# Making the MLP weight blocks elsewhere: none in the merge, two jobs fewer in the input stage, eight more in the first half of the MLP

## The chip, the cores and the metric

The kernel runs on one core of a Trainium2 chip. The metric is device time in microseconds (us). Before the change three runs took 2729.94, 2732.47 and 2736.2 us; the median is 2732.47.

The core has a matrix engine (PE, TensorE), and three engines for everything else: DVE (VectorE), ACT (ScalarE) and POOL (GpSimd). SP issues transfers; ACT and POOL can issue them as well. Matrix products land in PSUM banks and are taken out ("evicted") by DVE or ACT.

## What is computed

One layer of a transformer-like block on 2048 latent tokens of 1024 channels, with 256 context tokens. A token mixer (a Fourier part and a neighbourhood attention, gated and merged), then an MLP with a squared ReLU; both add to the residual stream. All is float32.

```python
hx = modulate(rms_norm(x, norm1_g), sh1, sc1)
fx, qx, kx, vx = split_projection(hx @ w_in)
...
y_four = fourier_mix(fx)
y_attn = neighbourhood_attention(qx, kx, vx, kc, vc, rpb)
mixed = gated_merge(hx, y_four, y_attn, w_branch_gate, w_fourier_out, w_attn_out, w_out)
x = x + g1 * mixed
hx2 = modulate(rms_norm(x, norm2_g), sh2, sc2)
a = relu(hx2 @ w_mlp1)          # 1024 -> 4096
x = x + g2 * ((a * a) @ w_mlp2) # 4096 -> 1024
```

## The kernel before

**Stages.** The program runs through the input projections (0 to about 850 us in the profiled execution), the Fourier transform along the tokens, attention (to about 1230), the merge (branch outputs, output projection, second norm; to 1530.8), and the MLP (to the end). Each float32 factor is split into a high and a low half of 16 bits, and a product is three matmuls (`mm3`, whose matmul stands on line 78).

**MLP.** Both matrix products are done by a Strassen-like scheme with 7 products in place of 8; a product is numbered c = 0 to 6. The tokens are cut in two halves. Each half goes through four groups of hidden channels (f = 0, 8, 16, 24). A group is a phase of the first product (mlp1: 4 units of 7 products, each of 12 matmuls, in PSUM tiles named pm) and then a phase of the second (mlp2: 7 products times 4 strips s of tokens, tiles named p): 336 matmuls of 128x512 each. In mlp1 every product is evicted by DVE or ACT into combinations u2, u3, u4, p1, which end as hidden tiles a (halves of 16 bits). In mlp2 it is added to accumulators X0 to X3 of its strip; the first one is written by ACT (line 1555), later ones are added by DVE (line 1551). mlp1 has four PSUM banks and mlp2 four others.

**Weight blocks.** The weights in this scheme are sums of quarters of the raw weight blocks. A *job* makes the 7 blocks of two neighbouring hidden tiles for w1 or w2: one load of raw weights (1 MB), 4 additions on DVE (`total`, line 414), and for each block a `put`: ACT makes the high half (line 375) and DVE the low half (line 376). Each block, 256 KB, is then stored to DRAM (w1d, w2d). There are 32 jobs. `prepare` is a generator that does one step at each `next`. Before the change 10 jobs are done in the input stage, at the end of the generator `side_work`, which `tick` advances between matmul groups there; 6 in the merge loop, whose steps stand between the parts of `out_proj` and `attn_out`; and 16 in the first half of the MLP, spread by the index of the product ("slot") up to a horizon. In the MLP there is one room for raw weights; the next 1 MB is fetched when a job is done. Its load is issued by ACT, the stores by POOL.

**Ring.** In both halves the MLP reads the blocks back through a ring of 15 tiles (wb), loaded by SP (line 1543) in the order of use. `issue_after` keeps the loads in this order. A load waits until PE is through with the tile that it overwrites.

**Normalised input.** The second norm writes its tiles (ho) to DRAM (hcd, line 1432), and the MLP reads the 7 combinations of them as tiles hc of 1 MB (line 1511): four (c = 0, 5, 6, 4) before the last token tiles are done, three (c = 1, 3, 2) after `norm_T` of the last tile has been issued in the program.

**Order.** Each engine runs its instructions in the program's order as a scheduler has placed them; transfers start in the order in which their issuing engine comes to them.

**The tail.** In the last group of a half the results are scaled (g2r), added to x (xr) and stored. The order of products in mlp2 is 0, 1, 4, 5, 2, 6, 3, so that c = 6 with six DVE instructions for each strip is next to last and c = 3 with two is last.

Of the kernel before, what the change touches and what calls it, by code (L numbers as in the profile page):

```python
# [8 lines left out]
F32 = mybir.dt.float32  # L9
# [10 lines left out]
D = 1024  # L20
# [16 lines left out]

PRODUCTS = (0, 5, 6, 4, 1, 3, 2)
PRODUCTS2 = (0, 1, 4, 5, 2, 6, 3)


# [18 lines left out]
def dit_block(ctx: ExitStack, tc: tile.TileContext, a, out, taps=None, upto=9):  # L60
# [223 lines left out]
    def side_work():  # L284
# [67 lines left out]
        for i, top in enumerate((BTOP, BTOP, BTOP, ATOP)):  # L352
# [8 lines left out]
        dve.tensor_scalar(out=g2r, in0=g2r, scalar1=msc[:, 4:5], scalar2=None, op0=ALU.mult)  # L361
        yield

        yield from prepare(jobs[:N_EARLY], lambda n_: pb.tile([128, KT, 256], F32, tag="awt", name=n_, bufs=2).rearrange("p k n -> p (k n)"),
                           lambda n_: pb.tile([128, 2, 256], F32, tag="aacc", name=n_, bufs=2).rearrange("p a n -> p (a n)"),
                           lambda n_: pb.tile([128, D], F32, tag="xh", name=n_, bufs=5)[:, :512].bitcast(F16).rearrange("p (o n) -> p o n", o=2),
                           sp.dma_start, sp.dma_start, True)
        del jobs[:N_EARLY]


    prepared, N_EARLY, N_MERGE = set(), 10, 6
    jobs = [(kind, f + o) for f in range(0, FF // 128, 8) for kind in (1, 2) for o in range(0, 8, 2)]
# [4 lines left out]

    def prepare(todo, raw_room, sum_room, out_room, load_, dma, ahead):

        todo, raws, out_ = list(todo), {}, []  # L380

# [14 lines left out]
        for n, (kind, f) in enumerate(todo):  # L396
# [8 lines left out]

            def put(c, src):
                flush()
                o = out_room(f"wo{nm}_{c}")
                d = o.rearrange("p o (k n) -> p o k n", k=4) if kind == 1 else o
                halve(d[:, 0], d[:, 1], src, msc[:, 0:1] if kind == 1 else msc[:, 2:3])  # L410
                out_.append(((w1d, w2d)[kind - 1][f // 2][c], o.rearrange("p o n -> p (o n)")))

# [4 lines left out]
            if kind == 1:  # L417
                order = ((0, b11, ()), (4, s3, (b21, b22, ALU.add)), (5, s3, (s3, b11)), (1, b12, ()), (6, b21, (b11, b21)),
                         (3, b22, ()), (2, s3, (b12, s3)))
            else:  # L420
                order = ((0, b11, ()), (4, s3, (b12, b11)), (5, s3, (b22, s3)), (2, b22, ()), (6, b12, (b22, b12)),
                         (1, b21, ()), (3, s3, (b21, s3)))
            for j, (c, o, ops) in enumerate(order):
                if ops:
                    total(o, *ops)
                put(c, o)
# [73 lines left out]
    def unit_T(wu, h, dst, m0, tk, func, name):  # L500
        w, u = wu
        for m in range(2):
            ps = mmp.tile([128, 512], F32, tag="mm", name=f"ps_{name}_{m}")
            ms = slice(m * 128, (m + 1) * 128)
            mm3(ps, [(w[:, 0, k, ms], w[:, 1, k, ms], h[:, 0, k], h[:, 1, k]) for k in range(KT)])
            put_T(ps, dst, m0 + m, tk, func, f"{name}_{m}", u[:, 1:2])
            tick()
            yield
# [31 lines left out]
    def unit_qk(wu, h, qk, p0, tk, t_rope, name):  # L540
# [66 lines left out]
        for i in range(nt):  # L607
            turned.append((back, i, front(i)))
            turn(3)
            tick()  # L610
            yield
# [6 lines left out]
    def unit_v(wu, h, u, tt, name):  # L618
        w, sc = wu
        und = sc[:, 1:2] if tt < 16 else sc[:, 2:3]  # L620
        for i in range(h.shape[3] // 128):
# [8 lines left out]
            sp.dma_start(vF[tt + i, :, u * 256:(u + 1) * 256], vo)  # L630
            tick()
            yield
# [228 lines left out]
    for n in range(len(seq)):  # L861
# [7 lines left out]
        if n == len(seq) - 1:  # L869
            for o in beside:  # L870
                for _ in o:
                    pass
# [596 lines left out]
    load_x1()  # L1469
    rooms = []  # L1470

    def block_room(i):

        if not rooms:
            rooms.append(pm.tile([128, 4, 512], F32, tag="mL", name="wrooms"))
        t = rooms[0][:, i]
        return t.bitcast(F16).rearrange("p (o n) -> p o n", o=2) if i else t

    turns = iter(range(1000))
    prep = prepare(jobs[:N_MERGE], lambda n_: pm.tile([128, 2048], F32, tag="mH", name=n_), lambda n_: block_room(0),  # L1480
                   lambda n_: block_room(1 + next(turns) % 3), sp.dma_start, pool.dma_start, False)
    for t in range(NT - 2):
        out_proj(t, 0)
        if t:
            next(prep, None)
        out_proj(t, 1)
        for _ in attn_out(t + 2, mmp, pg):
            if t:
                next(prep, None)
        if t:  # L1490
            next(prep, None)
        norm_T(t)
    for _ in prep:
        pass
    del jobs[:N_MERGE]
    pm.release()
# [20 lines left out]
    for half in range(2):  # L1517
        for f in range(0, NF, GF):
            pairs = tuple(range(f, f + GF, 2))
            slots += [(1, half, f1, c) for f1 in pairs for c in PRODUCTS]  # L1520
            slots += [(2, half, f, 0, s, pairs[:-1]) for s in range(4)] + [(2, half, f, 0, s, pairs[-1:]) for s in range(4)]
            slots += [(2, half, f, c, s, pairs) for c in PRODUCTS2[1:] for s in range(4)]

# [10 lines left out]
    def load_block():  # L1534
# [7 lines left out]
        with tc.issue_after(ring_load[0].ins) if ring_load[0] else nullcontext():  # L1542
            ring_load[0] = sp.dma_start(t.rearrange("p o n -> p (o n)"), (w1d, w2d)[kind - 1][f // 2][c])

# [100 lines left out]
    prep = prepare(jobs, lambda n_: pr.tile([128, 2048], F32, tag="raw", name=n_), lambda n_: pr.tile([128, 512], F32, tag="wt", name=n_),  # L1645
                   lambda n_: small(n_).bitcast(F16).rearrange("p (o n) -> p o n", o=2), act.dma_start, pool.dma_start, False)
    acc, banks = {}, {}

    def mlp2(half, f, c, s, pairs):
# [152 lines left out]
```

## Time and profile before

| | us |
|---|---|
| median of three runs | 2732.47 |
| the profiled execution | 2738.39 |
| its span | 2736.6 |
| PE busy | 2572.6 (94%) |
| DVE busy | 1813.5 (66%) |
| ACT busy | 1180.4 (43%) |
| POOL busy | 456.7 (17%) |
| mean granted clock of PE | 0.977 of full speed |

The profiled execution is one of its own; its span is the time between the first and last instruction on the core. A line of a wait says which engine stood idle before which instruction (output tile and line), and what ended the idle time. Releasers are inferred from semaphores: where an engine waits for several things, the last one is named. The times of all rows are those of this one execution.

### The profile page before, as it was taken

The page shows a single profiled execution, that of the slowest core. Times are in us where ns is not written, and L with a number is a line of the kernel's source. Part 1 is how long each engine was busy: PE and PEld are TensorE (multiplying, and loading weights), DVE is VectorE, ACT ScalarE, POOL GpSimd, SP SyncE. Part 2 cuts the span into 40 slices and gives each one's busy share as a digit, 9 for nine tenths or more (in the row PEclk, how much of TensorE's full clock was granted, in tenths as well). Part 3 has the DMA queues.
Part 4 walks back from the last instruction along what each step waited for, and adds up shares of the span by engine and source line. Part 5 has one row for each costly group of instructions (what it writes and reads, how often), then busy time and mean ns, then how long its engine had stood idle before and what let it go on. Part 6 is the DMA issues. An engine that isn't in the chain of part 4 may idle for free.

```text
span 2736.6 us, 42696 instructions
## 1 busy us (share of the span) xinstructions
PE 2572.6 (94%) x15825; PEld 1567.7 (57%) x15825; DVE 1813.5 (66%) x3628; ACT 1180.4 (43%) x2105; POOL 456.7 (17%) x688
## 2 busy tenths in 40 slices
PE   6899988898999799988999799999999999999998
PEld 5445756776746588877888444444444444444444
DVE  7746974667652678887896484877766743636367
ACT  5623326545331678873553372625342242414050
POOL 1201211012234454432120011111110100000000
PEclk9999999999999999999999999999999999999999
DMA  8577789777354655457987656655556533333334
GB/s 262 149 221 199 219 251 292 255 230 243 102 168 116 165 142 163 139 160 238 309 286 267 217 183 209 195 196 189 200 192 239 194 99 105 96 108 93 112 100 142
DMA packets 345514, 509.38 MB, mean 186 GB/s; under 512 B 48753, under 2 KB 210761, under 8 KB 340953
## 3 DMA queue, kind: packets, MB, share of 16 engines
q1 hardware_dynamic: 301897, 410.17, 48.2%
q0 software_dynamic: 27424, 69.72, 7.7%
q10 hardware_dynamic: 15984, 26.76, 3.0%
q8 instruction: 124, 2.03, 0.3%
q14 instruction: 85, 0.70, 0.1%
HBM read 361.72 MB, written 145.84 MB: 185 GB/s over the span
## 4 chain that ended last, share of the span: by engine, by line
PE 62%; DMA 14%; DVE 13%; issue 4%; ACT 4%; SPq 2%; POOL 1%; ACTq 0%; DVEq 0%; POOLq 0%
PE p L78 19%; PE pm L78 16%; PE ps_g L78 8%; PE po L78 4%; DMA w12m<-in_w_mlp 4%; DMA raw<-in_w_mlp 4%; PE tp L1259 2%; PE ps_k L78 2%; PE pmf L1197 2%; PE ps_f L78 2%; PE pv L1273 2%; SPq L178 1%; PE sc L1237 1%; PE pua L78 1%; DVE wo L376 1%
## 5 line engine op out<-in xcount | busy, mean ns | idle before, releaser
L78 PE MATMUL pm<-hc,wb 128*128 128x512 f16 x2688 | 585.5, 381 | 17.1 <-DMA hc<-hcd 12.5
L78 PE MATMUL p<-wb,a 128*128 128x512 f16 x2688 | 584.9, 380 | 10.4 <-DVE X L1551 5.5
L78 PEld LDWEIGHTS <-wb 128*128 128x128 f16 x2688 | 263.7, 98 | 337.3 <-issue 23.1
L78 PEld LDWEIGHTS <-a 128*128 128x128 f16 x2688 | 263.7, 98 | 330.3 <-issue 15.3
L78 PE MATMUL ps_g<-hx,w_g 128*128 128x512 f16 x1536 | 342.5, 380 | 0.7 <-ACT ot_f L497 0.7
L1551 DVE TENSOR_TENSOR X<-X,p 128x512 f32<-128x512 f32 x280 | 184.2, 685 | 219.7 <-PE p L78 194.1
L78 PEld LDWEIGHTS <-hx 128*128 128x128 f16 x2304 | 230.0, 100 | 45.3 <-issue 9.4
L78 PEld LDWEIGHTS <-w_g 128*128 128x128 f16 x1536 | 150.9, 99 | 170.9 <-issue 2.7
L1551 DVE TENSOR_TENSOR u<-pm,u 128x512 f32<-128x512 f32 x128 | 87.9, 690 | 94.0 <-PE pm L78 91.6
L1025 POOL DMA_DIRECT2D bt<-tT x264 | 132.4, 508 | 79.0 <-DVE ri L1266 58.7
L1246 DVE CUSTOM_DVE_ANT_0 s<-sc,bt,qsc 128x736 f32<-128x736 f32 (+5 forms) x128 | 111.2, 869 | 38.6 <-PE sc L1240 35.1
L1555 ACT ACTIVATE p<-pm 128x512 f32<-128x512 f32 x32 | 19.0, 593 | 253.5 <-PE pm L78 253.5
L375 ACT ACTIVATE wo<-raw,msc 128x512 f16<-128x512 f32 x104 | 71.6, 712 | 114.1 <-DMA raw<-in_w_mlp 67.8
L78 PE MATMUL po<-wouH,mH 128*128 128x512 f32 x256 | 103.0, 405 | 15.2 <-DVE ga L1316 15.2
L375 ACT ACTIVATE wo<-ws,msc 128x512 f16<-128x512 f32 x78 | 56.2, 720 | 140.6 <-DVE ws L414 91.3
L1267 DVE SCALAR_TENSOR_TENSOR pL<-tp,pH 128x640 f16<-128x640 f32 (+1 forms) x128 | 112.3, 877 | 6.7 <-ACT pH L1262 6.5
L497 ACT ACTIVATE ot_g<-ps_g,usc_g 128x512 f32<-128x512 f32 x64 | 43.6, 683 | 169.3 <-PE ps_g L78 155.4
L1682 POOL DMA_DIRECT2D xr<-x1d x32 | 17.3, 539 | 569.3 <-DVE X L1551 562.6
L1250 ACT ACTIVATE s<-s,m 128x736 f32<-128x736 f32 (+5 forms) x128 | 104.4, 816 | 15.9 <-DVE m L1246 15.5
L1259 PE MATMUL tp<-ident,s 128*128 128x128 f32 x704 | 104.3, 282 | 2.2 <-ACT s L1250 2.0
L78 PE MATMUL po<-wouH,mL 128*128 128x512 f32 x256 | 102.2, 401 | 0.0
L78 PE MATMUL po<-wouL,mH 128*128 128x512 f32 x256 | 102.2, 400 | 0.0
(511 smaller groups left out, 4778.5 us busy)
## 6 DMA issues: line engine op xcount, KB each, us to landing
wb<-w1d SPq DMA_DIRECT2D x224, 256.0 KB
wb<-w2d SPq DMA_DIRECT2D x224, 256.0 KB
w12m<-in_w_mlp SPq DMA_DIRECT2D x32, 1024.0 KB
gT<-ot_g SPq DMA_DIRECT2D x64, 256.0 KB
raw<-in_w_mlp SPq DMA_DIRECT2D x16, 1024.0 KB
raw<-in_w_mlp ACTq DMA_DIRECT2D x16, 1024.0 KB
hc<-hcd SPq DMA_DIRECT2D x14, 1024.0 KB
w1d<-wo POOLq DMA_DIRECT2D x56, 256.0 KB, 2.7
```

Of the source, the lines that this page charges most:

```text
L78: last_mm[0] = pe.matmul(ps, l, r, start=(start and i == 0), stop=(stop and i == n - 1))
L178: last_load[0] = sp.dma_start(dst, src)
L375: act.activation(hi, src, AF.Copy, scale=scale)
L497: act.activation(o, ps, func, scale=scale)
L1025: load_(t[i * 16:(i + 1) * 16, :, off + j0 * w:off + (j0 + 8) * w], raw(tT[ct], (2 * hp * 15 + dr) * w, [[120 * w, 16], [15 * w, 2], [1, 8 ...
L1197: pe.matmul(ps, l, r, start=(i == 0), stop=(i == len(prods) - 1))
L1246: tail["dve"] = dve.tensor_tensor_reduce(out=s[:, :n], in0=sc, in1=bias, op0=ALU.add, op1=ALU.min, scale=qsc[:, 4:5], scalar=3.0e38, accum ...
L1250: tail["act"] = act.activation(s[:, :n], s[:, :n], AF.Exp, bias=m1[:, 0:1], scale=-1.0, accum_out=m1[:, 1:2])
L1259: tail["pe"] = pe.transpose(tp[:, i * 128:(i + 1) * 128], s[:, o:o + 128], ident)
L1267: tail["dve"] = dve.scalar_tensor_tensor(out=pL[:, :c], in0=tp[:, :c], scalar=PTOP, in1=pH[:, :c], op0=ALU.mult, op1=ALU.subtract)
L1273: tail["pe"] = pe.matmul(pv, p_[:nk, i * 128:(i + 1) * 128], vv[:nk, h2 * 128 + o:h2 * 128 + o + 64], start=(j == 0 and i == 0), stop=(j = ...
L1551: last["dve"] = dve.tensor_tensor(out=o, in0=x, in1=y, op=op)
```

## The change

No job is made in the merge any more. 8 jobs are made in the input stage by a generator of its own (`early_blocks`), which starts when the side work is through and is paced by shares given to `tick`; two blocks share a room and a store there, so a job takes 4 stores. 24 jobs are made in the first half of the MLP, spread by the matmuls of a slot (`cost`) in place of its index, with two raw rooms; the next raw weights are fetched at the second put of a job. Blocks lie in DRAM in the order in which they are made (`MADE`). The ring has 13 tiles. The three late hc loads come ahead of the ring loads that follow (`ring_load` is set to the last of them). The first X3 of a strip is written by DVE. In the last group the order of mlp2's products is 0, 4, 5, 2, 6, 1, 3.

```diff
+MADE = {1: (0, 4, 5, 1, 6, 3, 2), 2: (0, 4, 5, 2, 6, 1, 3)}
 PRODUCTS2 = (0, 1, 4, 5, 2, 6, 3)
+PRODUCTS2F = (0, 4, 5, 2, 6, 1, 3)
...
-        yield
+    def early_blocks():
         yield from prepare(jobs[:N_EARLY], ...
-                           sp.dma_start, sp.dma_start, True)
+                           2, sp.dma_start, sp.dma_start)
-    prepared, N_EARLY, N_MERGE = set(), 10, 6
+    prepared, N_EARLY = set(), 8
...
-            def put(c, src):
-                flush()
-                o = out_room(f"wo{nm}_{c}")
+            def put(j, src):
+                if j % n_out == 0:
+                    flush()
+                    room[:] = [out_room(f"wo{nm}_{j}")]
+                    end = min(j + n_out, 7)
+                    out_.append(((w1d, w2d)[kind - 1][f // 2][j:end].rearrange("c p n -> p c n"), room[0][:, :end - j]))
+                o = room[0][:, j % n_out].rearrange("p (o n) -> p o n", o=2)
...
-                if j == 1 and ahead:
+                if j == 1:
                     fetch(n + 1)
                 yield
-            if n + 1 == len(todo):
-                flush()
-            elif not ahead:
-                fetch(n + 1)
-                yield
+        flush()
...
+    blocks = [early_blocks(), 0.0, False]
-    def tick():
+    def tick(share):
...
                 for o in beside:
-                    next(o, None)
+                    if next(o, o) is o and o is side:
+                        blocks[2] = True
+            if blocks[2]:
+                blocks[1] += share
+                while blocks[1] >= 1.0:
+                    blocks[1] -= 1.0
+                    next(blocks[0], None)
...
-    prep = prepare(jobs[:N_MERGE], ..., sp.dma_start, pool.dma_start, False)
     for t in range(NT - 2):
         out_proj(t, 0)
-        if t:
-            next(prep, None)
         out_proj(t, 1)
         for _ in attn_out(t + 2, mmp, pg):
-            if t:
-                next(prep, None)
-        if t:
-            next(prep, None)
+            pass
         norm_T(t)
-    for _ in prep:
-        pass
-    del jobs[:N_MERGE]
...
-    RING, GF = 15, 8
-    def load_hc(half, part):
+    RING, GF = 13, 8
+    def load_hc(half, part, then=None):
...
-            sp.dma_start(r[c].rearrange("p s o k t -> p s (o k t)"), hcd[half][c])
+            i = sp.dma_start(r[c].rearrange("p s o k t -> p s (o k t)"), hcd[half][c])
+        if then:
+            then[0] = i
...
-    hcs[0].update(load_hc(0, 1))
+    hcs[0].update(load_hc(0, 1, ring_load))
...
-    prep = prepare(jobs, lambda n_: pr.tile([128, 2048], F32, tag="raw", name=n_), ...
+    prep = prepare(jobs, lambda n_: pr.tile([128, 2048], F32, tag="raw", name=n_, bufs=2), ...
...
-                acts(X[x], ps, scale=-1.0 if op == ALU.subtract else 1.0)
+                if (c, x) == (0, 3):
+                    last["dve"] = dve.tensor_copy(X[x], ps)
+                else:
+                    acts(X[x], ps, scale=-1.0 if op == ALU.subtract else 1.0)
...
-    todo, steps = 8 * len(jobs), 0
-    horizon = next(i for i, s in enumerate(slots) if s[:4] == (2, 0, NF - GF, 0)) - RING
+    todo, steps, done = 7 * len(jobs), 0, 0
+    cost = [4 if s[0] == 1 else len(s[5]) for s in slots]
+    horizon = sum(cost[:next(i for i, s in enumerate(slots) if s[:4] == (2, 0, NF - GF, 0)) - RING])
...
-            while steps * horizon < i * todo and next(prep, "end") is None:
+            done += cost[i]
+            while steps * horizon < done * todo and next(prep, "end") is None:
                 steps += 1
```

On SP, at the passage from the merge to the MLP, these instructions stand in a row before the change: the last stores of x (x1d), four ring loads (wb) of the unit f = 4, and the first two of the late hc loads (hc0_1 is c = 1 of the first half).

```order
L1400 DMA x1d_76<-x1_1792_18434 128x1024
L1400 DMA x1d_76<-x1_1920_18497 128x1024
L1543 DMA wb1_0_4_5_18883<-w1d2_81 128x1024
L1543 DMA wb1_0_4_6_18885<-w1d2_81 128x1024
L1543 DMA wb1_0_4_4_18893<-w1d2_81 128x1024
L1543 DMA wb1_0_4_1_18900<-w1d2_81 128x1024
L1511 DMA hc0_1_18877<-hcd0_77 128x4096
L1511 DMA hc0_3_18879<-hcd0_77 128x4096
```

In the changed kernel the same place on SP reads so (line numbers are those of the changed kernel):

```order
L1412 DMA x1d_76<-x1_1792_18149 128x1024
L1412 DMA x1d_76<-x1_1920_18212 128x1024
L1503 DMA hc0_1_18592<-hcd0_77 128x4096
L1503 DMA hc0_3_18594<-hcd0_77 128x4096
L1503 DMA hc0_2_18596<-hcd0_77 128x4096
L1538 DMA wb1_0_2_2_18598<-w1d1_80 128x1024
L1538 DMA wb1_0_4_0_18606<-w1d2_81 128x1024
L1538 DMA wb1_0_4_5_18615<-w1d2_81 128x1024
```

The hc loads have moved ahead of the ring loads, and the ring loads behind them are four blocks earlier in the stream.

On DVE, at the start of the MLP, the last tile of the norm (ho7) is followed before the change by these (raw1_16 are the first raw weights of the MLP, ws their sum, wo a block, pm0_0_1 the product c = 1 of the first unit, p1 where it is added):

```order
L1431 TENSOR_TENSOR ho7_1_18865<-tm7_18805,ho7_1_18865 128x512
L1551 TENSOR_TENSOR a0_0_3_18926<-a22_0_0_18804,a0_0_3_18926 128x512
L414 TENSOR_TENSOR ws1_16_18889<-raw1_16_18887 128x512
L376 SCALAR_TENSOR_TENSOR wo1_16_0_18890<-raw1_16_18887,msc_139,wo1_16_0_18890 128x512
L376 SCALAR_TENSOR_TENSOR wo1_16_4_18897<-ws1_16_18889,msc_139,wo1_16_4_18897 128x512
L1551 TENSOR_TENSOR p1_0_0_18746<-pm0_0_1_18907,p1_0_0_18746 128x512
```

And in the changed kernel:

```order
L1443 TENSOR_TENSOR ho7_1_18580<-tm7_18520,ho7_1_18580 128x512
L1546 TENSOR_TENSOR a0_0_3_18652<-a22_0_0_18519,a0_0_3_18652 128x512
L423 TENSOR_TENSOR ws1_8_18602<-raw1_8_18600 128x512
L423 TENSOR_TENSOR raw1_8_18600<-raw1_8_18600 128x4x128
L381 SCALAR_TENSOR_TENSOR wo1_8_0_18603<-raw1_8_18600,msc_139,wo1_8_0_18603 128x512
L381 SCALAR_TENSOR_TENSOR wo1_8_1_18610<-ws1_8_18602,msc_139,wo1_8_1_18610 128x512
L1546 TENSOR_TENSOR p1_0_0_18461<-pm0_0_1_18633,p1_0_0_18461 128x512
```

Four instructions in place of three that need the first raw weights stand ahead of the eviction of the product; the raw weights are now those of an earlier group, f = 8.

## Rows read from the trace of the kernel before

**Rows 1.** Windows of four stretches: busy us and instructions by engine, clock, DMA, GB/s.

```profile
490.00:720.00 230.00, 211.70 (x1580) 158.32 (x1578) 167.60 (x417) 109.43 (x195) 29.92 (x31) 0.96 0.70 227
...
1252.50:1530.80 278.30, 265.76 (x1457) 230.41 (x1458) 210.25 (x404) 130.35 (x223) 40.41 (x59) 0.97 0.80 273
...
1573.10:2003.90 430.80, 419.85 (x1921) 188.99 (x1921) 306.35 (x476) 193.50 (x307) 55.97 (x104) 0.99 0.60 195
2003.90:2729.00 725.10, 725.10 (x3360) 328.55 (x3358) 413.54 (x639) 216.49 (x343) 29.70 (x55) 1.00 0.42 133
```

**Rows 2.** Waits of PE, 490 to 720: us in total, times, longest.

```profile
PE pu_g L475 <- DVE usc_k L476: 7.6, 2, 4.3
PE ps_k0c L78 <- DVE qn_k L558: 5.3, 1, 5.3
PE ps_v L78 <- ACT vo_v L627: 3.1, 2, 1.8
```

**Rows 3.** Waits of PE, 1252 to 1530 us.

```profile
PE po L78 <- DVE ga L1316: 15.2, 5, 7.0
PE tpb L1418 <- DVE tm L1423: 3.6, 1, 3.6
```

**Rows 4.** Waits of PE, 1525 to 1945 us.

```profile
PE pm L78 <- DMA hc<-hcd: 12.5, 3, 9.9
PE p L78 <- DVE X L1551: 5.5, 2, 4.1
PE p L78 <- ACT X L1555: 4.9, 1, 4.9
PE pm L78 <- DVE p L1551: 4.0, 1, 4.0
```

**Rows 5.** Waits of DVE, 1252.5 to 1530 us.

```profile
DVE wrooms L414 <- DMA raw<-in_w_mlp: 11.6, 5, 3.7
...
DVE wrooms L376 <- ACT wrooms L375: 3.5, 6, 1.1
```

**Rows 6.** Chain that ended last: start us, us, what.

```profile
1276.92 7.87 DMA raw<-in_w_mlp
```

**Rows 7.** Timelines of the MLP's start: start, us, engine, line, instruction, idle before.

```profile
1533.45 8.09 SPq L1543 DMA_DIRECT2D wb<-w1d  x4
1547.53 8.12 SPq L1511 DMA_DIRECT2D hc<-hcd  x3
...
1554.06 4.29 PE L78 MATMUL pm<-hc,wb 128*128 128x512 f16 x12 [9.92 <-DMA hc<-hcd]
...
1557.09 0.52 ACTq L387 DMA_DIRECT2D raw<-in_w_mlp  x1
...
1570.17 0.69 DVE L414 TENSOR_TENSOR ws<-raw 128x512 f32<-128x512 f32 x1 [11.16 <-DMA raw<-in_w_mlp]
...
1572.33 0.68 DVE L1551 TENSOR_TENSOR p<-pm,p 128x512 f32<-128x512 f32 x1
1572.92 0.68 DVE L414 TENSOR_TENSOR ws<-ws,raw 128x512 f32<-128x512 f32 x1
```

**Rows 8.** Timeline of DVE: two puts in a row, in the merge.

```profile
1292.22 0.75 DVE L376 SCALAR_TENSOR_TENSOR wrooms<-wrooms,msc 128x512 f16<-128x512 f32 x1
1292.88 0.75 DVE L376 SCALAR_TENSOR_TENSOR wrooms<-raw,msc,wrooms 128x512 f16<-128x512 f32 x1
```

**Rows 9.** Timeline of PE: the longest stall of the merge.

```profile
1252.52 0.77 PE L78 MATMUL po<-wouH,mH 128*128 128x512 f32 x1 [6.98 <-DVE ga L1316]
```

**Rows 10.** Waits of DVE, 1573 to 2003.9 us.

```profile
DVE wo L376 <- ACT wo L375: 32.5, 28, 3.3
```

**Rows 11.** Waits of ACT, 1690 to 2003 us.

```profile
ACT wo L375 <- DMA raw<-in_w_mlp: 32.8, 7, 5.8
```

**Rows 12.** Timelines of PE and DVE at the end.

```profile
2719.82 9.23 PE L78 MATMUL p<-wb,a 128*128 128x512 f16 x42
...
2732.39 0.69 DVE L1551 TENSOR_TENSOR X<-X,t 128x512 f32<-128x512 f32 x1
```

More of the change, by code (lines that the diff above doesn't have):

```diff
@@ L361, in side_work @@
         dve.tensor_scalar(out=g2r, in0=g2r, scalar1=msc[:, 4:5], scalar2=None, op0=ALU.mult)
[L362 removed]
+    def early_blocks():
         yield from prepare(jobs[:N_EARLY], lambda n_: pb.tile([128, KT, 256], F32, tag="awt", name=n_, bufs=2).rearrange("p k n -> p (k n)"),
                            lambda n_: pb.tile([128, 2, 256], F32, tag="aacc", name=n_, bufs=2).rearrange("p a n -> p (a n)"),
[L366 to L367 removed]
+                           lambda n_: pb.tile([128, D], F32, tag="xh", name=n_, bufs=5).bitcast(F16).rearrange("p (c n) -> p c n", c=2),
+                           2, sp.dma_start, sp.dma_start)
         del jobs[:N_EARLY]
[L371 removed]
+    prepared, N_EARLY = set(), 8
     jobs = [(kind, f + o) for f in range(0, FF // 128, 8) for kind in (1, 2) for o in range(0, 8, 2)]
@@ L376, in halve, with prepare @@
         dve.scalar_tensor_tensor(out=lo, in0=src, scalar=scale, in1=hi, op0=ALU.mult, op1=ALU.subtract)
-    def prepare(todo, raw_room, sum_room, out_room, load_, dma, ahead):
-        todo, raws, out_ = list(todo), {}, []
+    def prepare(todo, raw_room, sum_room, out_room, n_out, load_, dma):
+        todo, raws, out_, room = list(todo), {}, [], []
         def fetch(n):
@@ L417, in prepare @@
             if kind == 1:
-                order = ((0, b11, ()), (4, s3, (b21, b22, ALU.add)), (5, s3, (s3, b11)), (1, b12, ()), (6, b21, (b11, b21)),
-                         (3, b22, ()), (2, s3, (b12, s3)))
-            else:
-                order = ((0, b11, ()), (4, s3, (b12, b11)), (5, s3, (b22, s3)), (2, b22, ()), (6, b12, (b22, b12)),
-                         (1, b21, ()), (3, s3, (b21, s3)))
-            for j, (c, o, ops) in enumerate(order):
+                order = ((b11, ()), (s3, (b21, b22, ALU.add)), (s3, (s3, b11)), (b12, ()), (b21, (b11, b21)), (b22, ()), (s3, (b12, s3)))
+            else:
+                order = ((b11, ()), (s3, (b12, b11)), (s3, (b22, s3)), (b22, ()), (b12, (b22, b12)), (b21, ()), (s3, (b21, s3)))
+            for j, (o, ops) in enumerate(order):
                 if ops:
                     total(o, *ops)
-                put(c, o)
+                put(j, o)
                 if j == 0 and n:
                     prepared.add(todo[n - 1])
-                if j == 1 and ahead:
+                if j == 1:
                     fetch(n + 1)
                 yield
-            if n + 1 == len(todo):
-                flush()
-            elif not ahead:
-                fetch(n + 1)
-                yield
+        flush()
         prepared.add(todo[-1])
@@ L506, in unit_T @@
             put_T(ps, dst, m0 + m, tk, func, f"{name}_{m}", u[:, 1:2])
-            tick()
+            tick(1.5)
             yield
@@ L609, in unit_qk @@
             turn(3)
-            tick()
+            tick(0.6)
             yield
@@ L630, in unit_v @@
             sp.dma_start(vF[tt + i, :, u * 256:(u + 1) * 256], vo)
-            tick()
+            tick(0.8)
             yield
@@ L869, in dit_block @@
         if n == len(seq) - 1:
-            for o in beside:
+            for o in beside + blocks[:1]:
                 for _ in o:
@@ L1469, in dit_block @@
     load_x1()
[L1470 to L1481, printed above, removed]
     for t in range(NT - 2):
         out_proj(t, 0)
-        if t:
-            next(prep, None)
         out_proj(t, 1)
         for _ in attn_out(t + 2, mmp, pg):
-            if t:
-                next(prep, None)
-        if t:
-            next(prep, None)
+            pass
         norm_T(t)
-    for _ in prep:
-        pass
-    del jobs[:N_MERGE]
     pm.release()
@@ L1521, in dit_block @@
             slots += [(2, half, f, 0, s, pairs[:-1]) for s in range(4)] + [(2, half, f, 0, s, pairs[-1:]) for s in range(4)]
-            slots += [(2, half, f, c, s, pairs) for c in PRODUCTS2[1:] for s in range(4)]
+            slots += [(2, half, f, c, s, pairs) for c in (PRODUCTS2 if f + GF < NF else PRODUCTS2F)[1:] for s in range(4)]
     def blocks_of(s):
@@ L1639, in dit_block @@
     p2p = psum("mlp2", 4)
-    hcs[0].update(load_hc(0, 1))
+    hcs[0].update(load_hc(0, 1, ring_load))
     def small(name):
         return pr.tile([128, 512], F32, tag="wo", name=name, bufs=5)
-    prep = prepare(jobs, lambda n_: pr.tile([128, 2048], F32, tag="raw", name=n_), lambda n_: pr.tile([128, 512], F32, tag="wt", name=n_),
-                   lambda n_: small(n_).bitcast(F16).rearrange("p (o n) -> p o n", o=2), act.dma_start, pool.dma_start, False)
+    prep = prepare(jobs, lambda n_: pr.tile([128, 2048], F32, tag="raw", name=n_, bufs=2), lambda n_: pr.tile([128, 512], F32, tag="wt", name=n_),
+                   lambda n_: small(n_).bitcast(F16).rearrange("p (c n) -> p c n", c=1), 1, act.dma_start, pool.dma_start)
     acc, banks = {}, {}
```

3 lines of the change are left out of this document (1 added, 2 removed).

## Prediction, made before the changed kernel was run

> **What bounds the kernel now.** I read the windows first [rows 1]. From 2003.9 us to its end TensorE (PE) never waits: 3360 matmuls in 725.1 us, 0.2158 us each, so a phase of 336 lasts 72.5 us. Nothing done before 2003.9 can shorten that, except the few us behind PE's last matmul. What can go is PE's idle time before it. The waits of PE show where it lies near this change: 16 us in the input stage between 490 and 720 us [rows 2], 18.8 us in the merge [rows 3], and 27 us from the start of the MLP to 1945 us [rows 4]. In each the last releaser is an instruction of VectorE (DVE) or ScalarE (ACT), or one transfer. The chain and the waits of DVE then say what these engines were late with: raw weights and the blocks made of them [rows 5, 6].
>
> A stall costs more than its length. The twelve matmuls behind the 9.92 us stall took 4.29 us [rows 7]; at 0.2158 us they take 2.59. [...]
>
> **Input stage (two jobs fewer, evenly, fewer stores).** One block job is 7 puts (one ACT, one DVE instruction each), 4 DVE totals, a load of 1 MB and 1.75 MB of stores. Two puts on DVE start 0.66 us apart [rows 8], two plain operations 0.6 (1572.33 and 1572.92 in [rows 7]), so a job is 7 x 0.66 + 4 x 0.6 = 7.0 us of DVE. Two jobs less are 14 us of DVE, 14 puts of ACT and 5.5 MB, in a stretch where DVE is busy 168 of 230 us and DMA 70% [rows 1]; stores fall from 70 to 32. The waits on usc_k, qn_k and vo_v (16 us, and up to three clock losses, 5 us) are for short DVE and ACT instructions queued behind the block work. All of that but two clock losses is the one end, -18. The other is +4: the last jobs now stand nearer to the end of the stage, and one more stall like those of vo_v, with its clock loss, may come. I take -7, nearer the middle, since the side work that fills DMA there stays.
>
> **Merge (no jobs).** 6 jobs go: 42 us of DVE, and the 15.1 us that DVE stood waiting for raw weights and for ACT's half of a put [rows 5]. Of the 18.8 us, the longest stall, 7.0, ended at 1252.5 [rows 3, 9], and the first raw load that the chain runs through began at 1276.9 [rows 6]; that stall stays. Left are 15.2 - 7.0 + 3.6 = 11.8 us, and three clock losses, 5.1 us: at most -17. DVE is busy 210 of 278 us there and loses a fifth of it, and PE, which waits for its ga and tm, is busy 266 of the 278. The other end is -5, one stall with its clock loss: DMA is busy for 80% of the stretch, and what carries the tiles of this loop stays. I take -13, since the raw waits stood in front of PE's own evictions.
>
> **Start of the MLP.** PE waited 12.5 us for three tiles of normalised input (hc), 3 MB, and 4.0 us for p [rows 4]. The hc loads were issued from 1547.53 on, behind four block loads issued from 1533.45 on, each of which waits until PE is through with an older block [rows 7]. In the new order they stand ahead of those, right behind the last store of x, so they can start where the block loads did, 14 us sooner: the 12.5 us and one clock loss go. But what is late next is close. DVE's eviction of p (1572.33) stands behind three instructions that need the first raw weights, which landed at 1570.17, 13 us after their issue at 1557.09 [rows 7]. The new order has four there. PE has four banks and stops after as many products. The raw load's issue still stands behind the stores of the last norm tile. With hc out of the way those stores finish some 4 us sooner and the load needs about the 7.87 us of the chain [rows 6]: landing near 1561, 10 us earlier. From the landing to where the first mlp2 product needs its accumulator DVE has 104 instructions now, some 9 more, which is 5.4 us later. Net -5. The ends: -14, if the load's issue comes sooner with the shorter merge tail too; and +3, if the landing hardly moves.
>
> [...]
>
> **First half of the MLP (24 jobs where 16 were, two raw rooms).** 8 jobs more are 56 us of DVE, of which the order puts most where DVE has room: in the mlp2 phases, 48, 67, 68, 84 DVE instructions become 72, 85, 85, 84; in the mlp1 phases, 119, 100, 99, 82 become 128, 107, 109, 89. The first need at most 53 us of 72.5. The second bind: by 0.6 and 0.66 us they were 73, 62, 61 and 50 us and become 79, 66, 68 and 55, in a stretch of some 78 us (72.5 and what the banks let PE run ahead), and their ends were late by 4.9, 1.4 and 4.1 us already [rows 4]. The second and third group get 4.6 and 6.6 us more work. Against that stand DVE's waits for ACT's half of a put, 32.5 us, behind ACT's waits for raw weights, 32.8 us [rows 10, 11]: with a second room the next 1 MB is fetched two puts into a job instead of after it, 8 us or more ahead. I take 0 for the two groups; the ends are -5.5 (both late ends gone) and +11 (all waits stay, 4.6 + 6.6). DMA gets 8 x 2.75 MB more over 430 us, 195 to some 246 GB/s, in a stretch where it was busy 60%; at the merge's 273 GB/s it was 80%. The ring shrinks from 15 to 13 blocks; in mlp1 that is 13 x 2.59 = 34 us of lead, and in mlp2, with four in use, 9 x 2.59 = 23 us, against some 8 us for a load four times a block's size. I give it nothing.
>
> On what one DVE instruction costs, starts are 0.59 us apart (1572.33, 1572.92) while one lasts 0.68 [rows 7]. [...] The rows say that the next starts inside that time.
>
> **Tail.** PE ends at 2729.05 and DVE's last instruction at 2733.08 [rows 12]; it works off a queue, as the second to last product (c = 6) gives it 6 instructions in each strip, 4 x 6 x 0.6 = 14.5 us for 10.4 us of PE. Now a product with 3 (7.3 us) stands between that and the last one, and the queue is empty when the last begins: -2.5 (ends -0.5 and -2.7). The first X3 of each strip moves from ACT to DVE: some 20 instructions after 2003.9, where DVE is busy 414 of 725 us [rows 1]: nothing.
>
> **The sum** against the profiled execution's own 2738.4 us (span 2736.6 and 1.8 around it): -7 - 13 - 5 + 0 - 2.5 = -27.5, so 2710.9. That execution is 5.9 us above the median of the runs, 2732.5; on that basis 2705.
>
> **Rivals.** (a) *More than that.* Nothing is late next: merge -17, input -12, start -14, tail -2.5: -45.5, 2687. For it: every wait named has block work ahead of it in its engine's queue. Against: the norm tile's stores still stand before the raw load.
> (b) *The merge and the input stage were held by their own transfers.* DMA at 80% and 70% for it; DVE's waits for raw weights against it. Then 0 - 5 - 5 - 2.5: -12.5, 2720. If the early jobs are not done by the ticks and are drained in one go ahead of attention, it comes to the same number.
> (c) *Slower: block work on DVE and ACT sets the pace of the first three mlp1 phases.* 24 jobs where 16 were, and if each put waits for ACT as long as now, 32.5 us become 49, +16; all waits stay, +11; the start's gain is used up, +5; three stalls more than 3 us long lose the clock, +5. Together +37 on the forecast, 2742. For it: DVE has 66 to 79 us of work in 78. Against: two raw rooms. It decides from some 27 us of new waits on DVE or ACT between 1560 and 1950 us. [...] I count it here, with a chance of 0.03, since the starts speak against it.
>
> **How the numbers follow.** Forecast 0.50 (own range 2695 to 2716), (a) 0.15, (b) 0.18, (c) 0.17. A difference of 0.2%, 5.5 us, is about what a measurement can tell. Faster: the first three less a few hundredths, 0.80; within: those and a part of (c), 0.07; slower 0.13. The range, 2686 to 2738, reaches to (a) and up to (b) with the unknown ends of the MLP's terms (+3, +11).
>
> **What would show it.** In the merge no waits of DVE on raw, and PE's waits on ga and tm after 1277 mostly gone. No wait of PE on hc; the three loads issued right behind the last store of x; the first raw weights landing some 10 us closer behind PE's first mlp1 product. At the first mlp2 product of the first three groups PE waits of 5 us or less. No PE wait on wb, and none in the second half. DVE's last instruction 1 to 2 us behind PE's. It is wrong if the merge keeps over 8 us of such waits, or if PE's waits on X, u and p between 1560 and 2000 us exceed 20 us.

## The result

The changed kernel takes 2700.35 us (median of 4 runs, 2696.91 to 2706.24) against 2733.02 before (median of 4, 2729.94 to 2736.2): ratio 0.9883, 95% interval 0.9862 to 0.9904. It is 32.7 us faster; the forecast was 2705, and the range held it. The profiled execution took 2706.24 us, with a span of 2704.4.

The two profiled executions, cut at the same places of the program (us):

| stretch | forecast | before | after | difference |
|---|---|---|---|---|
| start to PE's first output projection behind the 7 us stall | -7 | 1252.5 | 1247.6 | -4.9 |
| from there to PE's first mlp1 product (merge) | -13 | 278.3 | 258.2 | -20.1 |
| first group of the MLP | -5 | 175.7 | 176.9 | +1.2 |
| second and third group | 0 | 297.3 | 291.4 | -5.9 |
| from there to PE's last matmul | 0 | 725.2 | 725.2 | 0 |
| PE's last matmul to DVE's last instruction | -2.5 | 4.0 | 1.5 | -2.6 |

So the total came out near the forecast, and not all of its terms did: the merge gave 7.1 us more than forecast and the second and third group 5.9 more, the start of the MLP 6.2 less and the input stage 2.1 less. These misses largely cancel, so that the total lies 5 us from the forecast is in part luck. Of the signs that the prediction named, those on the hc loads and on the landing of the raw weights failed.

### The profile page after: what moved, and what is told of

Same layout as the page of the kernel before. It is cut to its first block, busy times and chain, and to the rows that moved or that the text cites. A ratio compares the mean times of both kernels' runs of the same rounds, so it can differ in the third digit from the quotient of the medians.

```text
span 2704.4 us, 42578 instructions
## 1 busy us (share of the span) xinstructions
PE 2563.6 (95%) x15825; PEld 1564.8 (58%) x15825; DVE 1813.9 (67%) x3636; ACT 1169.9 (43%) x2097; POOL 462.6 (17%) x702
## 4 chain that ended last, share of the span: by engine, by line
PE 71%; DMA 11%; DVE 10%; ACT 3%; issue 2%; POOL 1%; SPq 1%; ACTq 0%; DVEq 0%; POOLq 0%
PE p L82 21%; PE pm L82 19%; PE ps_g L82 8%; PE po L82 7%; DMA w12m<-in_w_mlp 4%; PE pua L82 3%; PE tp L1271 2%; PE ps_k L82 2%; PE pmf L1209 2%; PE pv L1285 2%; DMA raw<-in_w_mlp 1%; PE sc L1249 1%; PE ps_f L82 1%; DMA vF<-vo_v 1%; DVE wo L381 1%
## 5 line engine op out<-in xcount | busy, mean ns | idle before, releaser
L380 ACT ACTIVATE wo<-ws,msc 128x512 f16<-128x512 f32 x96 | 68.9, 718 | 152.2 <-DVE ws L423 119.6
L380 ACT ACTIVATE wo<-raw,msc 128x512 f16<-128x512 f32 x128 | 87.8, 710 | 66.1 <-issue 25.5
L1262 ACT ACTIVATE s<-s,m 128x736 f32<-128x736 f32 (+5 forms) x128 | 104.4, 816 | 13.1 <-DVE m L1258 12.4
```

The costliest lines, as they stand in the source:

```text
L380: act.activation(hi, src, AF.Copy, scale=scale)
L1262: tail["act"] = act.activation(s[:, :n], s[:, :n], AF.Exp, bias=m1[:, 0:1], scale=-1.0, accum_out=m1[:, 1:2])
```

## The profile after

Windows of the changed kernel, with the columns of [rows 1] (span of the stretch; busy us of PE, its weight loads, DVE, ACT and POOL; clock, DMA share, GB/s): the merge, the first three groups of the MLP, and the rest.

```profile
1247.60:1505.80 258.20, 258.18 (x1456) 226.20 (x1456) 171.13 (x338) 104.68 (x181) 15.22 (x17) 0.99 0.65 223
...
1505.80:1682.70 176.90, 152.87 (x689) 68.37 (x689) 128.01 (x203) 87.35 (x146) 28.26 (x52) 0.95 0.73 245
1682.70:1827.80 145.10, 145.10 (x674) 65.78 (x673) 121.93 (x193) 71.30 (x116) 27.59 (x51) 1.00 0.75 247
1827.80:1974.10 146.30, 145.19 (x674) 65.74 (x673) 123.19 (x194) 71.04 (x116) 28.57 (x53) 1.00 0.76 247
...
1974.30:2699.40 725.10, 725.10 (x3360) 328.56 (x3358) 422.82 (x656) 218.46 (x345) 32.95 (x61) 1.00 0.43 137
```

In the merge PE is busy all the time: 12.5 us of idle time are gone. Its busy time itself fell by 7.6 us, from 265.8 to 258.2. Part of that is the clock. Before the change the granted clock of PE was 0.50 of full speed in three places of the merge, behind stalls of 4.8, 3.6 and 2.6 us:

```profile
1332.00:1335.00 3.00, 3.00 (x7) 2.36 (x8) 3.00 (x7) 0.94 (x3) 0.00 (x0) 0.50 1.03 400
1373.00:1376.00 3.00, 3.00 (x11) 2.51 (x11) 3.00 (x8) 2.59 (x5) 0.21 (x1) 0.50 0.78 244
1448.10:1451.10 3.00, 3.00 (x9) 2.33 (x8) 2.68 (x8) 2.06 (x4) 0.00 (x0) 0.50 0.42 130
```

Matmuls of 512 columns start some 0.43 us apart there (1332.44 and 1332.87), and 0.23 us apart right behind these places (1335.40 and 1335.63). Summed over the three that is some 5 us, an estimate from these starts. After the change the clock in the merge is full from 1251 us on. What the remaining 2.5 us or so of busy time are is not shown.

In the second group PE never stops, with DVE at 122 of 145 us, and DMA moves 247 GB/s, where 246 had been worked out.

Waits of PE, first in the merge (1245 to 1520 us; it answers to [rows 3]), then at the start of the MLP (1500 to 1940; [rows 4]).

```profile
PE po L82 <- DVE ga L1328: 7.1, 1, 7.1
PE tpb L1430 <- DVE tm L1435: 1.0, 1, 1.0
```

```profile
PE pm L82 <- DMA hc<-hcd: 12.0, 3, 9.5
PE pm L82 <- DVE u L1546: 4.8, 4, 2.2
PE pm L82 <- DVE p L1546: 4.6, 2, 3.0
PE p L82 <- DVE X L1666: 1.6, 1, 1.6
PE p L82 <- DVE X L1546: 1.1, 1, 1.1
```

The wait of 7 us ahead of the merge stayed, as forecast, and all the others in the merge went (the 1.0 us on tpb lies behind the first mlp1 product). The wait on hc stayed too, 12.0 us for 12.5. The timelines at the start of the MLP (the rows answer to [rows 7]) and SP's waits (1490 to 1560 us) show why.

```profile
1522.70 8.40 SPq L1503 DMA_DIRECT2D hc<-hcd  x3
...
1528.80 5.28 PE L82 MATMUL pm<-hc,wb 128*128 128x512 f16 x12 [9.49 <-DMA hc<-hcd]
...
1530.20 1.95 ACTq L1444 DMA_DIRECT2D hcd<-ho  x3
1532.17 4.46 ACTq L392 DMA_DIRECT2D raw<-in_w_mlp  x2
...
1544.28 0.69 DVE L423 TENSOR_TENSOR ws<-raw 128x512 f32<-128x512 f32 x1 [6.24 <-DMA raw<-in_w_mlp]
...
1546.94 0.68 DVE L1546 TENSOR_TENSOR p<-pm,p 128x512 f32<-128x512 f32 x1
```

```profile
SPq L1503 <- DMA hcd<-ho: 23.0, 3, 15.6
```

The hc loads stand first on SP, and yet they were issued 16.9 us behind PE's first mlp1 product (1505.8), as before (1547.5 against 1530.8). SP waited 15.6 us with the first of them for a store of a norm tile, which ACT had issued. In the trace of before SP waits in the same way at its hc loads, when the block loads ahead of them have already left (1525 to 1560 us; 13.1 us in three waits):

```profile
SPq L1511 <- DMA hcd<-ho: 13.1, 3, 6.8
```

The raw weights landed 38 us behind that product (39 before).

DVE's waits from 1500 to 1960 us answer to [rows 10] and, with the raw weights, to [rows 11]:

```profile
DVE wo L381 <- ACT wo L380: 24.2, 29, 1.7
...
DVE ws L423 <- DMA raw<-in_w_mlp: 6.2, 1, 6.2
```

After the first raw load no instruction of DVE waits for raw weights any more. At the end ([rows 12]) PE and DVE stop 1.5 us apart:

```profile
2659.80 39.66 PE L82 MATMUL p<-wb,a 128*128 128x512 f16 x183
...
2700.22 0.69 DVE L1546 TENSOR_TENSOR X<-X,t 128x512 f32<-128x512 f32 x1
```

## Experiments

Twelve kernels were run. All ratios are to the kernel before, run beside each; the time of an execution scatters by some 5 us, nearly all of it ahead of the merge, so the stages of the profile decide where the time alone can't.

**1. The jobs back in the merge.** The loop of the merge makes 6 jobs again, in the places of before; 18 are left for the MLP.

```diff
+    prep = prepare(jobs[:6], ..., 1, sp.dma_start, pool.dma_start, False)  # one raw room
     for t in range(NT - 2):
         out_proj(t, 0)
+        if t:
+            next(prep, None)
...
```

> The changed kernel with 6 of the jobs made in the merge again, with the steps where they stood before (18 jobs instead of 24 in the first half of the MLP). Theory: the merge's gain is due to these jobs alone, so the stretch from the merge's first output projection to PE's first mlp1 product goes from 258 back to about 278 us, and the time from 2700 to about 2716 to 2722 (the first half of the MLP, with 6 jobs less, gives back at most 4). Rival: the merge became shorter because the work ahead of it changed (fewer stores and blocks in flight when it starts); then the stretch stays under 265 us and the time under 2708.

Measured: 2714.26 us, ratio 0.9934 (0.9914 to 0.9955). The merge took 277.6 us (1232.4 to 1510.0). Waits of PE, then of DVE, in it:

```profile
PE po L82 <- DVE ga L1328: 16.3, 4, 7.1
PE tpb L1430 <- DVE tm L1435: 3.7, 1, 3.7
```

```profile
DVE wrooms L423 <- DMA raw<-in_w_mlp: 11.5, 5, 3.0
```

The jobs cost the merge 19.4 us, whatever comes ahead of it; the three groups of the MLP took 465.8 instead of 468.3 us with them gone. The theory holds for the merge and for what PE and DVE wait for there; the time is 2 us under its range.

**2. The hc loads in the old order on SP.**

```diff
-    hcs[0].update(load_hc(0, 1, ring_load))
+    hcs[0].update(load_hc(0, 1))
```

> The changed kernel with the three late hc loads in the old order on SP, behind the ring loads (the handing over of the last hc load is left out). Theory: the order on SP decides nothing, since an hc load waits until the stores of the last norm tile, which ACT issues, have landed; PE's wait on hc stays at 11 to 14 us and the time within 3 us of 2700. Rival: the order is worth what the prediction said, and PE's wait on hc, 12 us now, grows by 5 us or more, with the time at 2705 to 2712.

Measured: 2703.57 us, ratio 0.9892 (0.9873 to 0.9911), not to be told from 0.9883; the time is half a microsecond past the theory's range, the wait within it. Waits of PE from 1500 to 1950 us:

```profile
PE pm L82 <- DMA hc<-hcd: 12.0, 3, 9.9
```

The order on SP, on which my step rested, is worth nothing as long as ACT issues the stores. With the stores on POOL (the next experiment) the old order was not run; that it would cost something there is only argued: before, SP came to the end of the four block loads ahead of the hc loads 10.7 us behind PE's first product (1533.45 + 8.09 in [rows 7], against 1530.8).

**3. The stores of the last norm tile from POOL.**

```diff
-    norm_T(t + 1, act)
+    norm_T(t + 1, pool)
```

> The changed kernel with the stores of the last norm tile issued by POOL instead of ACT. Theory: the hc loads waited for these stores only because SP's and ACT's transfers take turns in one small set of completion semaphores; POOL's have another set. The hc loads are then issued some 10 us or more earlier relative to PE's first mlp1 product, PE's wait on hc falls from 12 us to under 4, and raw is issued earlier too; what is late next is the first raw weights, ahead of the eviction of p: net 5 to 12 us, 2688 to 2695. Rival 1: the hc loads wait for the room that the norm tiles leave, or for the data; then PE's wait on hc stays at 10 us or more and the time at 2697 to 2704. Rival 2: the wait on hc goes but the wait on p takes all of it: time as now.

Measured: 2685.36 us, ratio 0.9834 (0.9809 to 0.9858): 13 us faster than the changed kernel by the ratios, and under the range of the theory. Timelines at the start (PE's first mlp1 product at 1495.1), and SP's waits for such stores with the hc loads, and for raw weights with the ring loads (1480 to 1550 us):

```profile
1496.48 3.06 SPq L1503 DMA_DIRECT2D hc<-hcd  x3
...
1516.78 1.49 ACTq L392 DMA_DIRECT2D raw<-in_w_mlp  x2
...
1524.36 0.69 DVE L423 TENSOR_TENSOR ws<-raw 128x512 f32<-128x512 f32 x1 [4.68 <-DMA raw<-in_w_mlp]
...
1527.02 0.68 DVE L1546 TENSOR_TENSOR p<-pm,p 128x512 f32<-128x512 f32 x1
...
1527.76 4.56 PE L82 MATMUL pm<-hc,wb 128*128 128x512 f16 x14 [8.85 <-DVE p L1546]
```

```profile
SPq L1538 <- DMA raw<-in_w_mlp: 15.9, 2, 13.3
...
SPq L1503 <- DMA hcd<-ho: 0.4, 1, 0.4
```

The hc loads are issued 1.4 us behind PE's first product instead of 16.9, and PE no longer waits for hc. Neither the room nor the data held them, since both are as before. What held them is a completion semaphore. The trace of the changed kernel names the semaphore of each transfer and the times at which transfers raised it: SP's and ACT's transfers carry the same eight numbers (100 to 106 and 108), POOL's eight others (111 to 118). The first hc load had number 102 there, which a store that ACT issued at 1520.41 had just before it; that store's last raise of it came at 1522.63, and the load left at 1522.70. The other two left 0.02 us behind the last raise by stores of ACT with their numbers (1529.53 behind 1529.51 for 103, 1530.78 behind 1530.76 for 105). With the stores on POOL the first left at 1496.48, and SP's waits for them are the 0.4 us above. The ring loads behind them are still held in this way, by raw loads that ACT issues (13.3 us at the longest), but PE waits for none of them. What is late next is the eviction of p behind the four instructions on raw weights, 8.85 us. The first group takes 165.6 us, 11.3 less.

**4. And no block step before the ninth product.**

```diff
-            while steps * horizon < done * todo and next(prep, "end") is None:
+            while i > 7 and steps * horizon < done * todo and next(prep, "end") is None:
```

> As the run with the stores issued by POOL, and in addition no step of a block job before the ninth product of the MLP (the steps left out are made up after it), so that no instruction that needs raw weights stands ahead of the eviction of p. Theory: both waits at the MLP's start, hc and p, are gone; the time from PE's first mlp1 product to the end of the first group, 177 us now, is 158 to 165, and the whole 2682 to 2690. Rival: the block work made up later is late for the end of the first mlp1 phase, and PE waits there on X or on u for what was gained; then the whole is 2690 to 2700.

Measured: 2683.94 us, ratio 0.9822 (0.9803 to 0.9841); the first group 161.0 us. Waits of PE, 1494 to 1930 us:

```profile
PE pm L82 <- DVE p L1546: 4.7, 3, 2.4
PE pm L82 <- DVE u L1546: 4.5, 2, 2.3
```

The wait of 8.8 us is split into short ones, of which 4.6 us of the group are won. The two intervals overlap, so only the stage shows the gain, in one profile each. Time and stage lie in the range of the theory.

**5. One raw room in the MLP.**

```diff
-    prep = prepare(jobs, lambda n_: pr.tile(..., tag="raw", name=n_, bufs=2), ...
+    prep = prepare(jobs, lambda n_: pr.tile(..., tag="raw", name=n_), ...
...
-                if j == 1:
+                if j == 6:
                     fetch(n + 1)
```

> The changed kernel with one room for raw weights in the MLP instead of two; the next raw weights are fetched after the last put of a job. Theory: the second room is why the second and third group of the first half became 6 us shorter (145 and 146 us now, 147 and 151 before) although DVE got more work there; with one room ACT and DVE wait for raw weights again and these two groups together take 6 to 15 us more, the whole 2706 to 2716. Rival: the waits for raw weights were not on the path; the two groups change by less than 2 us and the time stays within 4 us of 2700.

Measured: 2732.39 us, ratio 0.9998 (0.9986 to 1.0009): the whole gain is gone. Waits of PE, then of DVE, 1500 to 1960 us:

```profile
PE pm L82 <- DMA hc<-hcd: 12.3, 3, 9.8
PE p L82 <- DVE X L1546: 10.0, 4, 3.3
PE pm L82 <- DVE p L1546: 8.0, 4, 3.7
PE pm L82 <- DVE u L1546: 7.7, 4, 3.8
```

```profile
DVE ws L423 <- DMA raw<-in_w_mlp: 56.5, 17, 11.1
DVE wo L381 <- ACT wo L380: 17.7, 20, 3.2
```

The four groups of the first half took 181, 160, 158 and 147 us instead of 177, 145, 146 and 145. The theory named the right room and a third of its price: DVE waits 56.5 us for raw weights, and what stands behind on DVE waits with it. The room and the earlier load go together here: with one room the next load can't come before the last put.

**6. X3 on ACT again.**

```diff
-                if (c, x) == (0, 3):
-                    last["dve"] = dve.tensor_copy(X[x], ps)
-                else:
-                    acts(X[x], ps, ...)
+                acts(X[x], ps, ...)
```

> The changed kernel with the first X3 of each strip written by ACT again instead of DVE. Theory: the waits of PE on X at the start of the mlp2 phases (4.9, 1.4 and 4.1 us before, 1.6, 0 and 1.1 now) were waits for an ACT that was behind with puts; with X3 on ACT they come back in part, and the three groups of the first half together take 2 to 8 us more. Rival: the shorter waits are due to the second raw room or to the spreading of the steps; then the three groups change by less than 2 us.

Measured: 2697.85 us, ratio 0.9858 (0.9835 to 0.9880). The three groups took 467.0 instead of 468.3 us: the rival's case, no effect.

**7. The old order in the last group.**

```diff
-PRODUCTS2F = (0, 4, 5, 2, 6, 1, 3)
+PRODUCTS2F = PRODUCTS2
```

> The changed kernel with the old order of mlp2's products in the last group (c = 6 next to last). Theory: DVE ends 4.0 us behind PE again instead of 1.5, so the time after PE's last matmul grows by 2.5 us and the rest stays. Rival: DVE's queue at the end has another cause, and the distance stays at 1.5 us.

Measured: 2698.6 us, ratio 0.9870 (0.9852 to 0.9888); its time can't tell 2.5 us. In the profile PE ends at 2691.28, and DVE's last instruction is

```profile
2694.62 0.69 DVE L1546 TENSOR_TENSOR X<-X,t 128x512 f32<-128x512 f32 x1
```

4.0 us behind PE, as before the change. The theory holds for the distance.

**8. The kernel before, with nothing but the jobs taken out of the merge.**

```diff
-    prepared, N_EARLY, N_MERGE = set(), 10, 6
+    prepared, N_EARLY, N_MERGE = set(), 10, 0
```

> The kernel before with one edit: the 6 jobs of the merge are made in the first half of the MLP (22 there), with one raw room, the old spreading and the old order of the hc loads. Theory: most of the whole gain is the merge's; the merge takes 258 us instead of 278, and the first half of the MLP gives back no more than 6 us; 2712 to 2720. Rival: without the second room and the new spreading the first half pays for the jobs (7 us of DVE each) in its mlp1 phases, 12 us or more in all; 2724 or more.

Measured: 2733.63 us, ratio 1.0005 (0.9988 to 1.0023). The merge took 258.0 us, and the four groups of the first half 177, 154, 156 and 152 where they took 176, 147, 151 and 145: 20 us won, 21 lost. DVE's waits, 1500 to 1960 us:

```profile
DVE ws L414 <- DMA raw<-in_w_mlp: 47.4, 12, 10.3
DVE wo L376 <- ACT wo L375: 22.7, 24, 4.1
```

The theory fell; this is the rival's case.

**9. The kernel before, with two raw rooms in the MLP (and 13 ring tiles to make space).** The steps of a job are counted as in the change, 7 for 8.

```diff
-    RING, GF = 15, 8
+    RING, GF = 13, 8
...
-    todo, steps = 8 * len(jobs), 0
+    todo, steps = 7 * len(jobs), 0    # and: bufs=2, next load at the second put
```

> The kernel before with two rooms for raw weights in the MLP, the next load at the second put, and for their space a ring of 13 blocks; jobs stay where they were (10, 6 and 16). Theory: the second room pays only where the jobs are many: with 16 jobs the raw waits cost at most what PE waited on X at the second and third group, 5.5 us and their clock losses, so the time is 2724 to 2731, 2 to 8 us less than before. Rival: the second room is the gain by itself, as much as with 24 jobs, where it was worth 32 us; then 2710 or less.

Measured: 2724.74 us, ratio 0.9982 (0.9970 to 0.9994). The three groups took 465.0 us, 8.0 less than before; PE's waits on X at the second and third group are gone (1520 to 1990 us):

```profile
PE p L78 <- ACT X L1555: 2.8, 1, 2.8
...
PE p L78 <- DVE X L1551: 0.4, 2, 0.2
```

The theory holds. With 16 jobs the second room is worth 8 us in these groups (4 us of the whole, whose interval is 2 to 8), with 24 jobs 32.

**10. Ten jobs in the input stage, evenly.**

```diff
-    prepared, N_EARLY = set(), 8
+    prepared, N_EARLY = set(), 10
```

> The changed kernel with 10 jobs in the input stage instead of 8, and 22 in the first half of the MLP. Theory: the two jobs cost the input stage up to 7 us, less what the first half of the MLP saves by having two less (0 to 2 us); 2700 to 2708, with DVE's later blocks in the input stage in front of the last q, k and v tiles. Rival: the number of jobs in the input stage is off the path of PE there; 2697 to 2702.

Measured: 2700.28 us, ratio 0.9887 (0.9870 to 0.9903), which lies in both ranges. The profile decides. From the transposition of the weight maxima (pms, at 484 to 497 us) to the first Fourier matmul (pc) three profiles with the input stage of before took 359.6, 357.3 and 354.8 us, nine with that of the change 348.9 to 355.5, mean 351.1, and this one 351.5. So the input stage won some 6 us, and as far as one profile tells not by making two jobs less. The three groups took 470.1 us with 22 jobs, no less than the 468.3 with 24.

**11. Both start edits, and the first raw load at once.**

```diff
         fetch(0)
+        if first:
+            yield
...
+    next(prep)          # in the MLP, before the loop over the products
```

> The changed kernel with the last norm tile's stores issued by POOL, no block step before the ninth product of the MLP, and the first raw load issued at once when the MLP begins, not with the first step. Theory: the first two jobs then have their raw weights when their steps are due, so the short waits on u and p in the first mlp1 phase (9 us in all in the run without the early load) shrink by 2 to 4 us: 2680 to 2685. Rival: these waits are DVE's load there and stay; 2682 to 2688.

Measured: 2682.88 us, ratio 0.9820 (0.9800 to 0.9840); the first group took 159.0 us, and the waits on u and p fell from 9.2 to 6.1 us (1490 to 1920):

```profile
PE pm L82 <- DVE u L1548: 4.0, 4, 2.1
PE pm L82 <- DVE p L1548: 2.1, 3, 0.8
```

The theory holds for the waits; the time is in both ranges.

**12. The same with 6 jobs in the input stage and 26 in the MLP.**

> As the run before, with 6 jobs in the input stage and 26 in the first half of the MLP. Theory: the first half has room for two more only in its mlp2 phases; its mlp1 phases are full, so it loses 4 to 12 us, more than the input stage gains (0 to 4): 2684 to 2694. Rival: the two rooms keep DVE ahead and the gain of the input stage stays: 2676 to 2682.

Measured: 2672.2 us, ratio 0.9786 (0.9771 to 0.9801), the fastest of all, 57 us less than the kernel before, run beside it (2729.11). The three groups took 448.9 us against 450.5 with 24 jobs: even 26 jobs cost the first half nothing. The input stage took 345 us in its one profile, under all nine with eight jobs (349 to 355.5), so from eight to six jobs it may have won something that from ten to eight it did not. Both of my expectations were too slow. Whether the last 10 us against the run before are all due to the two jobs is open: the two profiled executions took 2674.2 and 2674.5 us, and only the other runs differ.

## Why the prediction was right, and where it was not

**Input stage, -7: right in size, its cause not shown.** The two profiles gave -4.9 at the start of the merge; the stage by itself gave -6 over several. The start of the merge was at 1240.0 us on average over the nine profiles and at 1250.9 over the three with the input stage of before, 11 us later; the 5 us of it that lie outside the stage are not explained. I priced the term by 14 us of DVE for two jobs less; with all ten jobs the stage is as short, in one profile (experiment 10). What is left is the even spreading and the fewer, larger stores; these two were not told apart, and neither was run alone.

**Merge, -13: the mechanism right, the term too small, and the bound of -17 too.** All the stalls behind the first raw load went, 12.5 us of idle time by the windows (I had 11.8 from the waits). The clock term was right: three times 1.7 us in the prediction (by the twelve matmuls that took 4.29 for 2.59 us), three places at half clock worth some 5 us in the trace. But the busy time fell by 7.6 us, and the rest of that is in no term of mine. I had held 4 us back, since DMA at 80% might keep the loop's own tiles late; without raw weights and stores it is at 65%, and nothing waits. Experiment 1 gives 19.4 of the 20.1 us back. The bound of some 3 us, from which on a stall was to cost clock, is not sharp. In the trace of before, from 25 us on, the clock was at 0.50 within 1.3 us of the end of each of the 15 stalls of PE of 3.0 us or more, and behind shorter ones too, as the one of 2.6 us in the merge; in the changed kernel it stayed at 1.00 behind one of 3.3 us (477.9).

**Start of the MLP, -5: the step that failed.** "In the new order they stand ahead of those, right behind the last store of x, so they can start where the block loads did" is wrong. I took the hc loads to be held by the block loads ahead of them alone, and these wait for PE. The hc loads had a second condition, a completion semaphore that a store issued by ACT held. The trace of before had shown it, had I read SP's waits: 13.1 us of them at the hc loads, behind the last block load. Experiments 2 and 3 separate the two: the order alone changes nothing, and with the stores on POOL SP's wait for them falls from 23.0 to 0.4 us. The other half of the step, that raw weights ahead of the eviction of p are late next, shows in experiment 3 (8.85 us), and so does the landing of the raw weights, 29 us behind PE's first product instead of 38, which is the "10 us earlier". Then the term is -10 instead of +1.2. In that run two raw loads left ACT within 1.5 us of each other, and the first was there 7.6 us later, no later than the single load of [rows 6] (7.87). In the changed kernel the first raw load, issued by ACT while SP's hc loads were under way, was there 12.1 us after its issue (1532.17 to 1544.28); what made it longer is not shown.

**Second and third group, 0: at the end of its bound, -5.9 for -5.5.** I weighed the second room as a balance to 11 us of work, which put it too low. It is what the whole change stands on: without it the time is that of before (experiment 5), and experiments 8 and 9 show both halves, the jobs without the room (nothing won in all) and the room without the jobs (8 us in the stage). A DVE instruction that waits for raw weights holds every eviction behind it, and with one room there are 17 such waits, 56.5 us. The work itself, 122 us of 145, fits. The new spreading of the steps and the smaller ring were not run alone; with one room the first half loses with either spreading (experiments 5 and 8).

**Tail, -2.5:** measured -2.6, and +2.6 with the old order (experiment 7). X3's move cost nothing, and gave nothing (experiment 6).

**The rivals.** (c), block work that sets the pace of the mlp1 phases, is what happens with one room, but by another wait: I had priced it at 37 us, with DVE's waits for ACT's half of a put growing to 49 us; it is 32, and DVE waits 56.5 us for raw weights and only 17.7 for ACT. I gave it 0.17 as the second room spoke against it; that reason held. The 0.03 counted in it was for a DVE that takes the whole 0.68 us of an instruction before the next; no run shows one, and in the changed kernel the next starts 0.60 us later (1546.94 and 1547.54). (a) was right on the merge, and (b) nowhere that differs from the forecast.

## What to carry to other kernels

Work can be moved under a full matrix engine for nothing, as here to a DVE that is busy 122 of 145 us with it, if its inputs are there when its first instruction comes up on the shared engine: give it a second room before giving it more time. When a transfer is issued late, list all that it waits for, its completion semaphore too, and not only what stands ahead of it in its queue. And where a stall goes, count the matmuls at half clock behind it too; here they cost some 5 us beside 12.5 us of stalls.

## What the runs showed that I had not expected

- A load on SP was held for 15.6 us by stores that ACT had issued, through a completion semaphore of a set that the two share; stores issued by POOL did not do that (0.4 us), and the change of one word made the kernel 13 us faster (11.3 in the stage).
- The merge repeats within 2 us from execution to execution (257.8 to 259.4 us in all profiles without its jobs), while the same code ahead of it ended anywhere from 1232 to 1248 us. What a median of a few runs tells of an edit in the MLP is blurred by a stage that it does not touch.
